# Emitting each group's work in two lanes, and splitting the mixed features on ScalarE and VectorE, in a one-layer streaming encoder

## The chip, the core and the metric

The kernel runs on one core of one Trainium2 chip. The metric is the device time of one execution in microseconds (us). Five engines work side by side, each through its own instructions in a fixed order: PE (TensorE, matmuls; its weight loads are listed as PEld), DVE (VectorE), ACT (ScalarE), POOL (GpSimd) and SP (SyncE, which here issues most DMAs). An instruction whose inputs aren't ready holds up all that stands behind it on its engine.

## What is computed

One layer with three attention groups that read the same normalised input through one projection and are merged by one output projection. In the prompt part 2048 rows of width 1024 are processed; 8 short sequences of 16 new rows each ("samples") attend into caches.

```python
def reference(...):
    qa, ka, va, ga, qb, kb, vb, gb, qm, gm = split(rmsnorm(x, g_pre) @ w_in)
    oa = band_attention(qa, ka, va, 8 chunks of 64 to the left, learned bias by distance)      # 6 heads
    ob = band_attention(qb, kb, vb, 2 chunks to the left, ALiBi, sinks)                        # 6 heads, 2 kv heads
    om = softmax(qm @ mk.T) @ mv      # 4 heads, 256 memory tokens, mk/mv = rmsnorm(mem, g_mem) @ w_mem_kv
    o = concat([oa * silu(ga), ob * silu(gb), om * silu(gm)]) @ w_out
    y = x + rmsnorm(o, g_post)
```

Outputs are y for prompt and samples and the new keys and values. All is in float32. Every matmul operand is split into a high part (rounded to the matmul's format) and a low part (the rest), and a product is three matmuls: high by high, high by low and low by high.

## The kernel before

The prompt is worked on in four groups of 512 rows (g = 0 to 3; group 0 also carries the 128 sample rows). For each group the kernel projects the normalised columns `xn` into queries, keys, gates (`psT`, matmuls of 512 columns) and values (`psN`, 256 columns), computes attention a pair of heads at a time, multiplies each result with its gate into the mixed features `mo`, splits these into high and low part in `sh` (`mixhl`), and projects them out (`psN<-whl,sh`). Products with weights (`psT`, `psN`) are called dense here.

Attention of a pair of heads goes in steps over several engines. PE makes scores (`sa` for A, `sb_` for B, `sm` for M), DVE adds the bias and takes the row's extreme (L727, L798, L643), ACT takes the exponential (L729, L800, L648), DVE the reciprocal and the scaling (L731 and L732, L805 and L809, L650 and L653), PE transposes (`pt`, L247), ACT and DVE split the transposed weights into `sh` (L208, L209), PE multiplies with the values (`oa`, `ob`, `om`, L260), and ACT and DVE merge the two halves (`sums`, L267, L268). POOL applies the gate (L631).

PSUM is shared out by pools: two banks for dense products, one score tile of two banks, three tiles for transposes, one for attention outputs. So a second score tile waits until DVE or ACT has read the first.

The order of a group is written out by hand as a string of steps in `ORDERS`, each one a whole block: V (values), Pa and Pb (projections of a pair of heads), Aa, Ab and M (attention of a pair), Sa and Sb (samples), K (keys of B), X (reload of context), F (normalise, add and store the group before), N and L (scales and rows of the next group), Q (its M queries). After the string, at the group's end, come the split of the mixed features and the four quarters of the output projection, with the next group's M attention ahead of them in the text. A scheduler then orders each engine's instructions, with the place in the text as priority: where the instruction of the earlier block must wait, ready instructions of a later block go first, as far as buffers allow.

Weights arrive by DMA in `wraw`; ACT makes the high part of each (L139) and DVE and POOL in turn subtract it (L140). The mixed features are split by DVE and POOL:

```python
def split_mixed(dst, i, fs, src):
    dve.tensor_copy(dst[:, i, 0, fs], src)                                                      # L890
    pool.tensor_tensor(dst[:, i, 1, fs], src, dst[:, i, 0, fs].bitcast(F32), ALU.subtract)     # L891
```

`mixhl` lies over the keys, the values and part of the transposed weights in `sh`, so most of the split must wait until the group's attention has read them. In group 3 the first two quarters of the output projection leave out feature block 2 (the third A pair) and so start before that pair is done; in the code they stand after all attention.

In `split_q` (L214 to L220) a high part of the queries is also copied to the other half of the partitions: for head 0 by DVE, for head 1 by ACT (L220).

## Time and profile before

| | us |
|---|---|
| median of 3 runs | 1191.94 |
| lowest and highest | 1188.3 and 1194.71 |
| the profiled execution | 1191.06 |
| span of its trace, first to last instruction | 1189.3 |

| engine | busy us | share of the span |
|---|---|---|
| PE | 1132.3 | 95% |
| DVE | 838.6 | 71% |
| ACT | 690.3 | 58% |
| POOL | 351.4 | 30% |

A busy PE isn't a PE at its peak, since matmuls overlap. What can be read directly is the time in which PE is idle: 57 us of the span. The profile's chain of work that ended last is 71% PE and 17% DVE. The groups' ends lie near 330, 620, 890 and 1130 us.

### The profile page before, as it was taken

To read this page: it belongs to the slowest core of one execution; us is meant where nothing else is said; L and a number is where in the kernel's file an instruction comes from. 1 tells how busy PE (TensorE), PEld (TensorE's weight loads), DVE (VectorE), ACT (ScalarE), POOL (GpSimd) and SP (SyncE) were. 2 spreads that over 40 slices of the span, in tenths; PEclk is the share of its full clock that TensorE was granted. 3 is DMA by queue.
4 is the path that set the end of the run, shared out by engine and by line. 5 is a ranking of instruction groups with operands and counts; after the bars stand their busy time and mean duration, and the time that the engine had idled before them with its cause. 6 is when DMAs were issued, how large, how long until landed. Compare 5 with 4: busy or idle time off the path is not lost.

```text
span 1189.3 us, 20990 instructions
## 1 busy us (share of the span) xinstructions
PE 1132.3 (95%) x7794; PEld 1019.2 (86%) x7794; DVE 838.6 (71%) x1915; ACT 690.3 (58%) x1611; POOL 351.4 (30%) x280
## 2 busy tenths in 40 slices
PE   7999999998899999999989999999989998999897
PEld 6989898996689978898878988898778987988797
DVE  7849666777873547779997337679996336679965
ACT  7646565665634655558665455557764445567652
POOL 4212111111441651213333552122333451221541
PEclk9999999999989999999999999999999998999999
DMA  7772643525522683243311593334321471332213
GB/s 266 249 248 86 196 147 100 209 70 191 198 72 72 211 314 113 94 125 109 118 58 37 165 349 115 95 115 127 117 59 36 155 263 63 122 98 86 90 55 106
DMA packets 62238, 163.43 MB, mean 137 GB/s; under 512 B 8108, under 2 KB 19378, under 8 KB 62136
## 3 DMA queue, kind: packets, MB, share of 16 engines
q1 hardware_dynamic: 58392, 152.66, 38.6%
q0 software_dynamic: 3744, 9.44, 2.8%
q8 instruction: 61, 1.00, 0.3%
q14 instruction: 41, 0.34, 0.1%
HBM read 140.95 MB, written 23.48 MB: 138 GB/s over the span
## 4 chain that ended last, share of the span: by engine, by line
PE 71%; DVE 17%; ACT 4%; issue 3%; DMA 2%; POOL 1%; SPq 0%; DVEq 0%; POOLq 0%; ACTq 0%
PE psT L191 32%; PE psN L202 21%; PE pt L247 4%; PE oa L260 3%; PE sa L241 3%; DVE sh L209 3%; DVE sba L727 1%; DVE whl L140 1%; DVE sbm L653 1%; DVE sbb L809 1%; DVE sbb L798 1%; PE ss L358 1%; ACT whl L139 1%; PE ob L260 1%; PE so L392 1%
## 5 line engine op out<-in xcount | busy, mean ns | idle before, releaser
L191 PE MATMUL psT<-xn,whl 128*128 128x512 f32 (+2 forms) x2400 | 530.6, 370 | 11.9 <-ACT whl L139 7.4
L191 PEld LDWEIGHTS psT<-xn,whl 128*128 128x128 f32 x2400 | 409.7, 192 | 74.0 <-ACT whl L139 7.6
L140 POOL TENSOR_TENSOR whl<-wraw,whl 128x1024 fp32r<-128x1024 f32 x63 | 152.3, 2417 | 353.0 <-ACT whl L139 323.1
L202 PE MATMUL psN<-whl,sh 128*128 128x256 f32 x1296 | 162.1, 282 | 1.5 <-POOL sh L891 1.3
L202 PEld LDWEIGHTS psN<-whl,sh 128*128 128x128 f32 x1296 | 156.3, 189 | 3.4 <-POOL sh L891 1.5
L139 ACT ACTIVATE whl<-wraw 128x1024 fp32r<-128x1024 f32 (+1 forms) x132 | 138.0, 1047 | 31.0 <-PE psN L202 13.5
L202 PE MATMUL psN<-whl,xn 128*128 128x256 f32 x1080 | 142.9, 283 | 3.4 <-ACT stgN L618 1.1
L202 PEld LDWEIGHTS psN<-whl,xn 128*128 128x128 f32 x1080 | 133.1, 189 | 7.5 <-issue 1.6
L209 DVE TENSOR_TENSOR sh<-pt,sh 128x512 fp32r<-128x512 f32 (+2 forms) x206 | 123.8, 626 | 20.5 <-ACT sh L208 19.4
L208 ACT ACTIVATE sh<-pt 128x512 fp32r<-128x512 f32 (+2 forms) x206 | 104.4, 547 | 38.4 <-PE pt L247 32.5
L729 ACT ACTIVATE sba<-sba,sta 128x640 f32<-128x640 f32 (+4 forms) x96 | 73.1, 762 | 65.9 <-DVE sta L727 64.4
L140 DVE TENSOR_TENSOR whl<-wraw,whl 128x1024 fp32r<-128x1024 f32 (+1 forms) x69 | 99.0, 1435 | 16.4 <-ACT whl L139 15.9
L631 POOL TENSOR_TENSOR mo<-sums,gr 128x256 f32<-128x256 f32 (+1 forms) x44 | 44.8, 1019 | 187.8 <-DVE sums L268 179.9
L727 DVE CUSTOM_DVE_ANT_0 sba<-sa,nbA 128x640 f32<-128x640 f32 (+4 forms) x96 | 70.6, 735 | 31.3 <-PE sa L241 30.7
L260 PE MATMUL oa<-sh 128*128 128x256 f32 (+1 forms) x504 | 81.5, 283 | 10.9 <-DVE sh L209 7.6
L260 PEld LDWEIGHTS oa<-sh 128*128 128x128 f32 x504 | 71.1, 191 | 17.1 <-DVE sh L209 9.8
L497 DVE TENSOR_TENSOR mo<-psN,gpost 128x256 f32<-128x256 f32 x52 | 22.0, 424 | 74.2 <-ACT junk L496 74.1
L247 PE MATMUL pt<-ident,sba 128*128 128x128 f32 x420 | 66.6, 278 | 3.4 <-DVE sba L732 3.2
L800 ACT ACTIVATE sbb<-sbb,stb 128x256 f32<-128x256 f32 (+1 forms) x96 | 47.2, 493 | 27.4 <-DVE stb L798 27.2
L732 DVE TENSOR_SCALAR sba<-sba,sta 128x640 f32<-128x640 f32 (+4 forms) x96 | 59.9, 624 | 2.6
L496 ACT ACTIVATE junk<-psN 128x256 bf16<-128x256 f32 x52 | 20.0, 384 | 62.3 <-PE psN L202 62.1
L247 PEld LDWEIGHTS pt<-ident,sba 128*128 128x128 f32 x420 | 48.9, 142 | 7.1 <-DVE sba L732 4.2
(282 smaller groups left out, 1629.2 us busy)
## 6 DMA issues: line engine op xcount, KB each, us to landing
wraw<-in_wt SPq DMA_DIRECT2D x128, 512.0 KB, 3.8
xr<-in_x_p SPq DMA_DIRECT2D x16, 512.0 KB, 5.8
nbA<-skew_d SPq DMA_DIRECT2D x24, 320.0 KB, 3.3
vta<-in_cva SPq DMA_DIRECT2D x12, 512.0 KB, 4.5
xt<-in_x_p SPq DMA_DIRECT2D x12, 512.0 KB, 5.2
out_y_p<-mo SPq DMA_DIRECT2D x12, 512.0 KB, 4.8
vctx<-sh SPq DMA_DIRECT2D x9, 512.0 KB, 5.8
kctx<-sh SPq DMA_DIRECT2D x9, 512.0 KB, 4.0
```

The lines of the kernel that those rows point to most:

```text
L139: act.activation(hl[:, 0, m], raw[:, m], AF.Copy)
L140: eng.tensor_tensor(hl[:, 1, m], raw[:, m], hl[:, 0, m].bitcast(F32), ALU.subtract)
L191: pe.matmul(ps[:, :n], w[:, a, k * 128:(k + 1) * 128], src[:, b, k, c0:c0 + n], start=(i == 0), stop=(i == 23))
L202: pe.matmul(ps[:, :256], stat(a, k), w[:, b, (k % 4) * 256:(k % 4 + 1) * 256], start=(k == ks[0] and i == 0), stop=(k == ks[-1] and i == 2))
L208: act.activation(hi, src, AF.Copy)
L209: eng.tensor_tensor(lo, src, hi.bitcast(F32), ALU.subtract)
L247: pe.transpose(pt[:, i * 128:(i + 1) * 128], b, ident)
L260: pe.matmul(o[:, oc:oc + w], v, pt[:, part, c:c + w], start=(first and i == 0), stop=(i == n - 1), skip_group_check=True)
L727: dve.tensor_tensor_reduce(sb[:, :nk], s[:, c0:c0 + nk], nb[h][:, 640 - nk:], 1.0, 3.0e38, ALU.add, ALU.min, st[:, e:e + 1])
L729: act.activation(sb[:, :nk], sb[:, :nk], AF.Exp, bias=st[:, e:e + 1], scale=-1.0, accum_out=st[:, 2 + e:3 + e])
L732: dve.tensor_scalar(sb[:, :nk], sb[:, :nk], st[:, 4 + e:5 + e], 0.5, ALU.mult, ALU.mult)
L800: act.activation(dst, dst, AF.Exp, bias=st[:, i:i + 1], scale=-1.0, accum_out=st[:, 4 + i:5 + i])
```

## The change

1. Steps become generators that yield after a few instructions: a `psT` product after every 6 matmuls, a `psN` product after half its matmuls. A group's steps are given in two strings, `DENSE` and `ATTENTION`, and a loop emits them as two lanes: the dense lane gets a piece when its sum of costs is at most `PACE` = 0.3 of the attention lane's, or when attention has to wait for a step in `AFTER`. This changes the order of the text, and so the scheduler's priorities.
2. Attention goes head by head: `weigh` (scores to scaled weights) of one head, and beside it up to three pieces of `combine` (transposes, values, merge) of the head before. For A, head 0's merge is now emitted before head 1's transposes; before, both heads' merges came after both.
3. The output projection of a group (O0 to O3) becomes the start of the next group's dense lane. In group 3 the two early quarters (E0) follow the last projection Pa2 in the dense lane, beside the last attention pair.
4. `split_mixed` uses ACT for the high part and DVE for the subtraction. POOL has no part in it.
5. `split_q` copies both heads by ACT.
6. Buffers: bias tiles `nb` 2 to 3, weight tiles `sb` 5 to 6, gate slots 2 and 3 laid out apart, and `mom` (M features) a tile of its own, no longer the fifth row tile of `mo`.

The matmuls are the same 7521 in both programs, and so is the number of DMAs on SP (410).

```diff
-ORDERS = ("M0 M1 V0 Pa0 Sa0 Aa0 Pa1 Pb0 Aa1 K0 V1 Sb0 N0 Sa1 Ab0 Pb1 Ab1 Sb1 Pb2 Ab2 Pa2 Sb2 Sa2 Aa2 L0 Q0 Q1 C0",
-          "V0 F0 F1 M0 X0 Pa0 M1 Aa0 X1 Pa1 N0 Aa1 Pb0 K0 Pb1 V1 Ab0 Pb2 Ab1 Ab2 C0 Pa2 X2 L0 Aa2 Q0 Q1",
...
+DENSE = ("V0 Pa0 Pa1 V1 Pb0 K0 N0 Pb1 Pb2 Pa2 L0 Q0 Q1 C0",
+         "O0 O1 O2 O3 F0 F1 V0 X0 Pa0 Pa1 N0 Pb0 X1 K0 V1 Pb1 X2 Pb2 Pa2 L0 Q0 C0 Q1",
...
+         "O0 O1 O2 O3 F0 V0 X0 Pa0 Pa1 Pb0 X1 K0 V1 Pb1 X2 Pb2 Pa2 E0")
+ATTENTION = ("M0 M1 Sa0 Aa0 Sa1 Aa1 Sb0 Ab0 Sb1 Ab1 Sb2 Ab2 Sa2 Aa2",
+             "M0 M1 Aa0 Aa1 Ab0 Ab1 Ab2 Aa2",
...
+PACE = 0.3
+PIECE = 6
...
-    nbp = ctx.enter_context(tc.tile_pool(name="nbp", bufs=2))
-    sbp = ctx.enter_context(tc.tile_pool(name="sbp", bufs=5))
+    nbp = ctx.enter_context(tc.tile_pool(name="nbp", bufs=3))
+    sbp = ctx.enter_context(tc.tile_pool(name="sbp", bufs=6))
...
-            (act.copy if h else dve.tensor_copy)(q[x, h, c], q[m, h, c].bitcast(F32))
+            act.copy(q[x, h, c], q[m, h, c].bitcast(F32))
...
         def split_mixed(dst, i, fs, src):
-            dve.tensor_copy(dst[:, i, 0, fs], src)
-            pool.tensor_tensor(dst[:, i, 1, fs], src, dst[:, i, 0, fs].bitcast(F32), ALU.subtract)
+            act.activation(dst[:, i, 0, fs], src, AF.Copy)
+            dve.tensor_tensor(dst[:, i, 1, fs], src, dst[:, i, 0, fs].bitcast(F32), ALU.subtract)
...
+        lanes = [dense(), attention()]
+        spent, waits = [0, 0], [(), ()]
+        while any(lanes):
+            ready = [lanes[k] is not None and done.issuperset(waits[k]) for k in range(2)]
+            assert any(ready), (g, waits)
+            k = 0 if ready[0] and (not ready[1] or spent[0] <= PACE * spent[1]) else 1
+            got = next(lanes[k], None)
+            waits[k] = ()
+            if got is None:
+                lanes[k] = None
+            elif isinstance(got, (tuple, list)):
+                waits[k] = got
+            else:
+                spent[k] += got
```

What the scheduler makes of it is seen in the order of the instructions on each engine. First place: PE at the end of group 1, where its last attention pair (A, `sa` and `oa`) meets the output projection. Before, this stands there after the last dense matmuls (`psT`), and it goes on in this way for 16 more rows, to the first `psN<-whl,sh`; from the `psT` to there it is 94 matmuls of attention:

```order
L191 MATMUL psT<-xn,whl 128x512 x17
L260 MATMUL oa<-sh 128x256
L241 MATMUL sa<-sh,qr 128x320 x4
L260 MATMUL oa<-sh 128x256 x4
L247 MATMUL pt<-ident,sba 128x128 x4
L260 MATMUL oa<-sh 128x256 x3
L260 MATMUL oa<-sh 128x128 x4
L247 MATMUL pt<-ident,sba 128x128 x6
L241 MATMUL sa<-sh,qr 128x320 x4
L260 MATMUL oa<-sh 128x256 x5
```

With the change, from the last `psT` to the first `psN`, whole:

```order
L213 MATMUL psT<-xn,whl 128x512
L273 MATMUL pt<-ident,sba 128x128 x10
L267 MATMUL sm<-mK,qr 128x256 x8
L286 MATMUL oa<-sh 128x256 x8
L286 MATMUL oa<-sh 128x128 x4
L273 MATMUL pt<-ident,sba 128x128 x8
L267 MATMUL sm<-mK,qr 128x256 x8
L273 MATMUL pt<-ident,sba 128x128 x2
L286 MATMUL oa<-sh 128x256 x8
L286 MATMUL oa<-sh 128x128 x4
L226 MATMUL psN<-whl,sh 128x256 x25
```

The run of attention without a dense matmul between is 60 long where it was 94; the last scores of the A pair now stand ahead of it. The end of group 2 shows the same 60.

Second place: PE where group 3's last B pair (`ob`) meets its last A pair. Before, `psN<-whl,xn` being values or an early quarter of the output projection:

```order
L260 MATMUL ob<-sh 128x256 x6
L260 MATMUL ob<-sh 128x128 x2
L260 MATMUL ob<-sh,bv 128x128 x2
L241 MATMUL sa<-sh,qr 128x320 x4
L247 MATMUL pt<-ident,sba 128x128 x3
L241 MATMUL sa<-sh,qr 128x320 x4
L202 MATMUL psN<-whl,xn 128x256 x6
L260 MATMUL ob<-sh 128x256 x6
L260 MATMUL ob<-sh 128x128 x2
L260 MATMUL ob<-sh,bv 128x128 x2
L241 MATMUL sa<-sh,qr 128x320 x4
L247 MATMUL pt<-ident,sba 128x128 x7
```

With the change:

```order
L286 MATMUL ob<-sh,bv 128x128 x2
L226 MATMUL psN<-whl,xn 128x256 x6
L267 MATMUL sa<-sh,qr 128x320 x4
L226 MATMUL psN<-whl,xn 128x256 x6
L267 MATMUL sa<-sh,qr 128x320 x4
L273 MATMUL pt<-ident,sba 128x128 x3
L226 MATMUL psN<-whl,xn 128x256
L267 MATMUL sa<-sh,qr 128x320 x4
L226 MATMUL psN<-whl,xn 128x256 x15
L273 MATMUL pt<-ident,sba 128x128 x7
L226 MATMUL psN<-whl,xn 128x256 x14
```

The last B head is over before the A pair's scores begin, and dense matmuls stand between their steps: 42 in the first 15 rows after it, where 6 stood in 23 rows.

Third place: DVE at the end of group 1. Before, the casts of `split_mixed` (their subtractions stand on POOL), among the scalings of M's weights (`sbm`):

```order
L890 CAST sh<-mo 128x768 x2
L650 RECIPROCAL stm<-stm 128x2
L653 TENSOR_SCALAR sbm<-sbm,stm 128x256 x2
L209 TENSOR_TENSOR sh<-pt,sh 128x512
L653 TENSOR_SCALAR sbm<-sbm,stm 128x256 x2
```

With the change:

```order
L926 TENSOR_TENSOR sh<-mo,sh 128x768
L926 TENSOR_TENSOR sh<-mom,sh 128x256
L235 TENSOR_TENSOR sh<-pt,sh 128x512
L926 TENSOR_TENSOR sh<-mom,sh 128x256
L235 TENSOR_TENSOR sh<-pt,sh 128x512
L926 TENSOR_TENSOR sh<-mom,sh 128x256
L294 TENSOR_TENSOR sums<-oa,sums 64x256
L679 TENSOR_REDUCE stm<-sm 128x4
L926 TENSOR_TENSOR sh<-mo,sh 128x768 x2
L686 RECIPROCAL stm<-stm 128x2
L689 TENSOR_SCALAR sbm<-sbm,stm 128x256 x2
```

The subtractions now stand on DVE between the steps of attention, the last two ahead of a scaling of `sbm`; POOL's list has none.

## Rows read from the trace of the kernel before

**Rows 1.** The page's part 1: busy us, share of the span, instructions of each engine.

```profile
PE 1132.3 (95%) x7794; PEld 1019.2 (86%) x7794; DVE 838.6 (71%) x1915; ACT 690.3 (58%) x1611; POOL 351.4 (30%) x280
```

**Rows 2.** Stretches: from:to, length, busy us and instructions by engine, granted clock, DMA.

```profile
core 0: us, PE busy (x) PEld busy (x) DVE busy (x) ACT busy (x) POOL busy (x), PEclk, DMA share, GB/s
...
280.00:340.00 60.00, 51.42 (x330) 36.95 (x329) 47.70 (x107) 32.34 (x77) 27.39 (x24) 0.89 0.55 189
340.00:560.00 220.00, 219.09 (x1467) 199.76 (x1466) 138.69 (x305) 123.83 (x280) 67.12 (x46) 1.00 0.43 143
560.00:640.00 80.00, 72.32 (x469) 64.31 (x468) 74.36 (x156) 51.77 (x129) 28.72 (x26) 0.98 0.24 72
...
820.00:905.00 85.00, 75.79 (x484) 66.43 (x483) 81.19 (x176) 57.51 (x143) 30.59 (x28) 1.00 0.27 84
...
985.00:1000.00 15.00, 11.45 (x45) 9.04 (x44) 11.39 (x22) 7.54 (x15) 2.36 (x1) 0.77 0.22 71
...
1100.00:1136.00 36.00, 31.07 (x191) 26.96 (x190) 33.97 (x76) 23.26 (x50) 19.00 (x18) 0.95 0.23 75
```

**Rows 3.** PE in order of time, end of group 1: start, length, instruction, [idle before <-releaser].

```profile
596.09 4.12 PE L191 MATMUL psT<-xn,whl 128*128 128x512 f32 x17
...
610.95 0.35 PE L260 MATMUL oa<-sh 128*128 128x256 f32 x1 [1.52 <-DVE sums L268]
...
614.84 0.36 PE L202 MATMUL psN<-whl,sh 128*128 128x256 f32 x1
...
616.20 0.74 PE L260 MATMUL oa<-sh 128*128 128x256 f32 x4 [0.76 <-DVE sh L209]
...
621.82 0.30 PE L247 MATMUL pt<-ident,sbm 128*128 128x128 f32 x1 [0.57 <-DVE sbm L653]
...
630.25 0.33 PE L247 MATMUL pt<-ident,sbm 128*128 128x128 f32 x1 [0.97 <-DVE sbm L653]
632.05 0.90 PE L247 MATMUL pt<-ident,sbm 128*128 128x128 f32 x3 [1.48 <-DVE sbm L653]
```

**Rows 4.** DVE and POOL in order of time, the same place.

```profile
613.44 2.11 DVE L653 TENSOR_SCALAR sbm<-sbm,stm 128x256 f32<-128x256 f32 x2
...
616.07 0.60 DVE L653 TENSOR_SCALAR sbm<-sbm,stm 128x256 f32<-128x256 f32 x2
...
628.27 3.73 DVE L653 TENSOR_SCALAR sbm<-sbm,stm 128x256 f32<-128x256 f32 x2
...
613.11 2.02 POOL L891 TENSOR_TENSOR sh<-mo,sh 128x768 fp32r<-128x768 f32 x1 [1.30 <-PE pt L247]
...
627.97 3.88 POOL L891 TENSOR_TENSOR sh<-mo,sh 128x768 fp32r<-128x768 f32 x2 [0.68 <-DVE sh L890]
```

**Rows 5.** The subtraction from a transpose in PSUM, one line: min/median/max ns.

```profile
L209 DVE TENSOR_TENSOR sh<-pt,sh x206: 407/682/694, 99.9 to 1148.3; 128x512 fp32r<-128x512 f32 x82, 128x256 fp32r<-128x256 f32 x18, 128x384 fp32r<-128x384 f32 x3
```

**Rows 6.** Groups of like instructions: count, busy us, mean ns, idle before.

```profile
L220 DVE CAST qr<-qr 64x512 fp32r<-64x512 f32 x16 | 11.1, 691 | 0.5
L220 ACT CAST qr<-qr 64x512 fp32r<-64x512 f32 x16 | 9.9, 619 | 0.5
L890 DVE CAST sh<-mo 128x1024 fp32r<-128x1024 f32 x5 | 3.3, 699 | 1.1 <-POOL mo L631 1.1
L891 POOL TENSOR_TENSOR sh<-mo,sh 128x1024 fp32r<-128x1024 f32 x5 | 13.7, 2750 | 2.6 <-DVE sh L890 2.5
L139 ACT ACTIVATE whl<-wraw 128x1024 fp32r<-128x1024 f32 x130 | 136.8, 1054 | 29.1 <-PE psN L202 13.5 <-DMA wraw<-in_wt 7.7 <-PE psT L191 6.7
L140 DVE TENSOR_TENSOR whl<-wraw,whl 128x1024 fp32r<-128x1024 f32 x67 | 97.6, 1457 | 15.1 <-ACT whl L139 14.7
L140 POOL TENSOR_TENSOR whl<-wraw,whl 128x1024 fp32r<-128x1024 f32 x63 | 152.3, 2417 | 353.0 <-ACT whl L139 323.1 <-issue 25.6 <-PE sa L241 2.9
```

**Rows 7.** All engines in order of time, group 3, a stall away from a group's end.

```profile
991.66 2.36 POOL L140 TENSOR_TENSOR whl<-wraw,whl 128x1024 fp32r<-128x1024 f32 x1 [11.56 <-ACT whl L139]
...
991.98 2.40 DVE L732 TENSOR_SCALAR sba<-sba,sta 128x640 f32<-128x640 f32 x1
...
994.43 1.76 PE L247 MATMUL pt<-ident,sba 128*128 128x128 f32 x7 [1.67 <-DVE sba L732]
```

More of the change, by code (lines that the diff above doesn't have):

```diff
@@ L182, in loaded, with run @@
         return xk
+    def run(steps):
+        while True:
+            try:
+                next(steps)
+            except StopIteration as end:
+                return end.value
     def project_T(w, src, c0, n, ps=None):
@@ L758, in attn_a @@
-                sums = cp_.tile([128, 512], F32, tag="sums", name="sums")
-                for h in range(2):
-                    merge(o, h, 256 * h, sums, 256)
-                gate(pr, i0 * 128, 256, sums, G)
+                    s = p_s.tile([128, 1024], F32, tag="s", name="sa")
+                    scores(s, q, h, i * 128, segs)
+                    e = i - i0
+                    sb = sbp.tile([128, 640], F32, tag="sb", name="sba")
+                    dve.tensor_tensor_reduce(sb[:, :nk], s[:, c0:c0 + nk], nb[h][:, 640 - nk:], 1.0,
+                                             3.0e38, ALU.add, ALU.min, st[:, e:e + 1])
@@ L763, in project_b @@
+            return [(weigh(i0, h), combine(i0, h)) for i0 in (0, 2) for h in range(2)]
         def project_b(j0):
[L764 removed]
+            q, Q = yield from block_q(g, 3 + j0)
+            return q, Q, (yield from block_g(g, 3 + j0))
         def sample_b(j0, Q, G, ksm, vsm):
@@ L823, in attn_b @@
                     first = False
-                merge(o, h, 0, sums, 512)
-            gate(3 + j0, 0, 512, sums, G)
+                    yield 600
+                merge(o, h, 0, held["sums"], 512)
+                if h:
+                    gate(3 + j0, 0, 512, held["sums"], G)
+            return [(weigh(h), combine(h)) for h in range(2)]
         if g == 0:
@@ new lines, in out_quarter @@
+        def out_quarter(c):
+            nrt = 5 if g == 1 else 4
+            if c == 0:
+                turn["m"] = 1
+                for i in range(nrt):
+                    if g == 1:
+                        split_mixed(mixhl, i, slice(0, KB), mo[:, i])
+                    else:
+                        split_mixed(mixhl, i, slice(0, 6), mo[:, i, :6])
+                        split_mixed(mixhl, i, slice(6, KB), mom[:, :, i])
+                kept["post"] = gains()
+            ws = [weights("o", c, r) for r in range(2)]
+            for i in range(nrt):
+                yield from project_out(ws, c, i, *kept["post"])
+            if c == 3:
+                turn["m"] = 0
@@ new lines, in units, with attention, pieces @@
+        def units(what, j):
+            if what == "M":
+                return attn_m(j, *qg[j])
+            if what == "Aa":
+                return attn_a(j, pa[j][1], pa[j][3], at[j], vslots[j], vc[j])
+            if what == "Ab":
+                return attn_b(j, pb[j][0], pb[j][2], v3, bctx)
+            if what == "Sa":
+                return [(iter(()), sample_a(j, *pa[j][2:], pa[j][0], vsm[j]))]
+            return [(iter(()), sample_b(j, *pb[j][1:], kept["ksm"], vsm[3]))]
+        def attention():
+            last = None
+            def pieces(n):
+                nonlocal last
+                for _ in range(n):
+                    if last:
+                        cost = next(last[0], None)
+                        if cost is None:
+                            done.update(last[1])
+                            last = None
+                        else:
+                            yield cost
+            for step in ATTENTION[g].split():
+                while not done.issuperset(after(step)):
+                    if last:
+                        yield from pieces(1)
+                    else:
+                        yield after(step)
+                parts = units(step[:-1], int(step[-1]))
+                for i, (first, second) in enumerate(parts):
+                    for cost in first:
+                        yield cost
+                        yield from pieces(3)
+                    while last:
+                        yield from pieces(1)
+                    last = (second, [(g, step)] if i == len(parts) - 1 else [])
+            while last:
+                yield from pieces(1)
```

332 lines of the change are left out of this document (173 added, 159 removed), and 5 rows, old and new, of tables (ATTENTION, DENSE, ORDERS).

## The prediction

> **What bounds the kernel now.** I read the page's busy times first: PE is busy 95% of the span and DVE 71% [rows 1], and the 7521 matmuls stay, so a gain can only come out of PE's idle 57 us (1189.3 - 1132.3) and out of the time at the lower granted clock. Then I cut the span into stretches [rows 2]. From 340 to 560 us PE idles 0.9 of 220 us: away from the groups' ends nothing is to be had. The ends are different: idle 8.6 us in 280 to 340, 7.7 in 560 to 640, 9.2 in 820 to 905 and 4.9 in 1100 to 1136, **30.4 us** in all. In the same stretches the granted clock is 0.89, 0.98, 1.00 and 0.95 [rows 2]; as time at the half level (1.2 of 2.4 GHz), lost if PE had work all along, that is 0.11 x 60 + 0.02 x 80 + 0.05 x 36 = **10 us**. So about 40 us is the most that better group ends can give. Another 3.6 us of idle and 3.5 us of clock (0.23 x 15) lie in 985 to 1000, inside group 3.
>
> Third, PE in order of time at one end [rows 3]. From the last dense run, which begins at 596.09, to the first `psN` at 614.84 PE has attention alone, 94 matmuls in chains that go through DVE and ACT; five waits there and just after it make 5.3 of the 7.7 us: 1.52 for a merge (`sums`), 0.76 for a subtraction of transposed weights, and 0.57 + 0.97 + 1.48 = 3.0 for scaled M weights (`sbm`, L653). What holds DVE? It is busy 74.4 of 80 us there and 81.2 of 85 at the next end [rows 2]: full. And some of that is no work: two L653 take 0.60 us when POOL is quiet, 2.11 us while a `split_mixed` subtraction (L891) runs on POOL from 613.11, and 3.73 us beside the two of 627.97 [rows 4]. DVE work that reads a transpose out of PSUM isn't touched: 206 of them, none over 694 ns [rows 5]. So **a POOL subtraction stretches DVE work between SBUF tiles**, and at the group's end that is the work on which PE waits.
>
> **The change part by part.**
>
> *Split of the mixed features.* 17 row tiles of 1024 columns' worth. POOL loses five subtractions of 2750 ns and the narrower ones [rows 6], and nothing takes their place there; POOL isn't waited for much, so that is worth nothing by itself. DVE loses the cast (699 ns a tile) and gets a subtraction of the size of its weight subtraction, 1457 ns a tile [rows 6]: +0.76 x 17 = +13 us of DVE, some 3 us at each end. ACT gets a copy like its weight copy, 1054 ns a tile [rows 6]: 18 us on an engine that is busy 58% [rows 1]. The chain of one tile gets shorter, 1.05 + 1.46 = 2.5 us for 0.70 + 2.75 = 3.4, and four or five tiles in a row no longer queue on POOL. Against the +3 us at an end stand the stretched L653 that go away: 2.11 - 0.60 and 3.73 - 0.60 are 4.6 us for two rows alone [rows 4]. Queued behind the new copies on ACT are exponentials and copies of transposes, behind the new subtractions on DVE the next `sbm`; if nothing covers them, one tile's 2.5 us at each of four ends is 10 us, and if all is covered 0. I take 0, since the first tiles are ready before the last attention matmuls and their 24 dense matmuls stand behind them on PE.
>
> *Query copies to ACT.* 40 copies change engine: 16 wide ones are 11.1 us on DVE and 9.9 on ACT [rows 6]. With the same rates for the rest DVE loses some 22 us and ACT gains 21. In the quiet stretches this is free (ACT 124 of 220 us busy [rows 2]), at the ends it is 2 to 3 us off the full engine. With the split, DVE comes out at -22 + 13 = -9 us over the span, and its stretched work beside that.
>
> *Two lanes.* By the order, the macro position of attention hardly moves (scores stand within 10 us of dense work of where they stood), but the ends do: the run of attention without dense work is 60 matmuls where it was 94, 0.64 of it, at the ends of groups 1 and 2; in group 3 the last pairs have 42 dense matmuls among 40 of attention where 6 stood among 76. A's first head is merged before its second head's values, so the 1.52 us wait for `sums` [rows 3] halves. Nothing is paid for the pieces: a switch from dense to attention matmuls and back already happens all over 340 to 560 us, at 0.9 us idle [rows 2]. Added waits: POOL's gate of the last pair now stands behind the next bias tile's two fills, which wait for a DMA; behind the gate are the subtractions on DVE of tiles 2 and 3. I price that at 0, because the fills stood in that place before too; one more wait of a tile costs the 2.5 us above.
>
> *Buffers.* A third bias tile and a sixth weight tile let attention start earlier; between 0 and what the ends have left. I take 0 beside the order's gain.
>
> **The sum.** End of group 1, 7.7 us: `sbm` 3.0 goes whole, `sums` 0.8 of 1.5, of the remaining 3.1 a share of 0.36 (1 - 0.64) is 1.1: 4.9 saved, 64%. End of group 2 by the same share: 5.9 of 9.2. End of group 0: half its first 20 us is sample attention, which changes less; I take half, 4.3 of 8.6. End of group 3: two thirds of 4.9, 3.3, since dense work now stands in the gap. Idle saved: 18.4 us. Of the 10 us of clock I take half, 5, because the clock fell after PE had idled and more than half of the idle goes. Together **23.4 us**, against the profiled execution's own 1191.06: 1167.7, so **1168 us**. The median of the runs is 0.9 us above that execution, which is inside its spread.
>
> **The Trainium skill on POOL and DVE.** The trace shows L653 at 0.60, 2.11 and 3.73 us a pair by what POOL does [rows 4], and a PSUM operand immune [rows 5]. The Trainium skill, "SBUF — State Buffer", section on SBUF's two separate sides, states that VectorE and GpSimd share a port pair under an exclusive lock, held for a whole instruction, and that a VectorE operation with two SBUF inputs also loses against a GpSimd one that reads SBUF. The rows agree: the L653 of 613.44 ends 0.4 us after the L891 of 613.11. The rule speaks against one part of the change, since the new DVE subtraction has two SBUF inputs and POOL's weight subtractions read SBUF; by it the sum would be rival 2's 1187 instead of 1168.
>
> **The rivals.**
>
> 1. *Only the split counts.* The scheduler had already mixed dense work and attention, so lanes change the text more than the order. Then only what L891 stretched goes: 3.0 us at the ends of groups 1 and 2 each, as much together at the others, and a fifth of the clock, 2 us: 11 us, **1180 us**. For it: scores stand where they stood. Against: 60 for 94.
>
> 2. *The new subtraction is itself held up by POOL's weight subtractions.* They stay, 63 of 2417 ns [rows 6], and one of them held an L732 for 2.40 us and PE behind it for 1.67 [rows 7]. If at each end two of the subtractions lose 2.4 us and PE pays them, that is 4 x 2 x 2.4 = 19 us back: 1168 + 19 = 1187, **about no change**. For it: DVE is full at the ends. Against: dense matmuls stand behind the first tiles. The skill's rule above is a reason for it.
>
> 3. *Slower: finer mixing puts more attention in the way of weight subtractions.* PE takes its list in order, and a matmul of attention that waits for a held DVE step holds up the dense work behind it. Before, one such hit in 985 to 1000 us cost 3.6 us of idle and up to 3.5 of clock [rows 2, 7]. With single heads instead of pairs, less stands between a score and the use of its weights; group 3 now has `sa` twice in a row and `oa` at once behind it. At some 5 us a hit, five more hits eat the gain and six to seven make it slower than before by 0.5%: 1168 + 32 = **1200 us** with six to seven of the 63 subtractions. For it: 63 chances. Against: from 340 to 560 us, with its share of those 63, nothing of the kind shows.
>
> 4. *More than I give.* Attention that starts earlier leaves dense work for the ends, and all 40 us but 2 go, with 5 of the 985 stall: 1191 - 38 - 5 = **1148 us**.
>
> **How the numbers follow.** Forecast 1168: 0.53. Rival 1: 0.18, rival 2: 0.10, rival 3: 0.10, rival 4: 0.09. About 0.5% (6 us) is what a measurement of this kernel can tell from no change. Of the forecast 0.51 lies beyond it on the faster side, of rival 1 0.14 of 0.18, of rival 2 0.04 of 0.10, all of rival 4: faster 0.78; rival 3 leaves 0.08 on the slower side; the rest, 0.14, is the same. The range goes from rival 4's 1148, less 2 for its own spread, to the median of before, 1192: outside are rival 3 and a little of rival 4 and 2, some 0.15.
>
> **What would show it.** Right: PE idle under 14 us in the four ends together, no `sbm` scaling above 1 us beside a split, DVE's total near 825 us or below, ACT near 730, POOL near 300; the same quiet middle. Only the split: the long waits for `sbm` gone and those for `sums` and transposed weights as before. Rival 2: the subtractions of `split_mixed` at twice 1.4 us, with a weight subtraction on POOL beside them. Rival 3: new PE waits of over 1 us for `sba` or `sbb` in the middle of groups. Wrong altogether: PE idles away from the ends for weights or for a DMA.

## The result, and the profile after

The changed kernel takes **1179.5 us** (median; 1177.1 to 1180.0), the kernel before 1192.5 in the same comparison: a ratio of 0.988, 95% interval 0.986 to 0.990, or 13 us less. The prediction said 1168 in a range of 1146 to 1192: the direction holds and the range does, but the gain is 13 us where the sum said 23.4. The profiled execution took 1177.05 us, its span is 1175.3; those of before are 1191.06 and 1189.3.

Page of the changed kernel, part 1, to be read against [rows 1]:

```profile
PE 1126.3 (96%) x7794; PEld 1019.6 (87%) x7794; DVE 810.9 (69%) x1875; ACT 729.4 (62%) x1688; POOL 301.1 (26%) x243
```

PE's idle time fell from 57.0 to 49.0 us, and its busy time by 6.0 for the same matmuls. The totals that were forecast for the others (825 or less, 730, 300) came. Stretches of the changed kernel, to be read against [rows 2] (its groups end some microseconds earlier, so the last one is moved); columns are time, length, busy us and count by engine, granted clock, DMA share and rate:

```profile
core 0: us, PE busy (x) PEld busy (x) DVE busy (x) ACT busy (x) POOL busy (x), PEclk, DMA share, GB/s
0.00:80.00 80.00, 66.52 (x471) 61.86 (x471) 51.98 (x97) 49.67 (x101) 22.86 (x26) 0.96 0.72 239
...
205.00:220.00 15.00, 10.88 (x65) 8.87 (x64) 12.68 (x43) 10.71 (x32) 5.01 (x4) 0.77 0.50 160
280.00:340.00 60.00, 53.58 (x354) 41.04 (x353) 47.34 (x111) 38.99 (x87) 17.87 (x21) 0.94 0.53 180
340.00:560.00 220.00, 218.51 (x1474) 200.26 (x1473) 137.74 (x304) 129.32 (x288) 62.05 (x43) 1.00 0.42 141
560.00:640.00 80.00, 74.62 (x501) 66.96 (x500) 71.83 (x159) 62.52 (x151) 20.31 (x20) 1.00 0.24 77
...
820.00:905.00 85.00, 80.72 (x540) 72.40 (x539) 76.83 (x177) 66.34 (x161) 22.36 (x22) 1.00 0.27 87
...
1095.00:1130.00 35.00, 32.45 (x218) 30.11 (x218) 29.12 (x56) 27.11 (x59) 8.55 (x4) 0.90 0.28 93
```

And two stretches of the kernel before that the prediction did not look at:

```profile
0.00:80.00 80.00, 70.37 (x523) 65.06 (x524) 56.27 (x107) 50.10 (x102) 23.66 (x25) 0.98 0.75 246
205.00:220.00 15.00, 14.87 (x127) 12.21 (x128) 7.50 (x18) 6.89 (x16) 4.78 (x2) 1.00 0.87 317
```

The four ends did get better: idle 6.4, 5.4, 4.3 and 2.6 us, 18.6 for 30.4. But the first 80 us idle 13.5 for 9.6, and 205 to 220 us, which was full, idles 4.1 and runs at 0.77 of the clock.

PE at the end of group 1 in the changed kernel, to be read against [rows 3]:

```profile
567.12 1.22 PE L267 MATMUL sb__6329<-sh,xn 128*128 128x256 f32 x8 [1.00 <-DVE stb L856]
...
590.52 5.87 PE L213 MATMUL psT<-xn,whl 128*128 128x512 f32 x24 [0.66 <-DVE qr L245]
...
613.11 1.72 PE L273 MATMUL pt<-ident,sba 128*128 128x128 f32 x8 [1.29 <-DVE sh L235]
...
618.91 2.98 PE L226 MATMUL psN<-whl,sh 128*128 128x256 f32 x23 [1.06 <-DVE sh L926]
621.74 1.03 PE L273 MATMUL pt<-ident,sbm 128*128 128x128 f32 x8
```

The waits for scaled M weights (`sbm`, 3.0 us) and for the merge (1.5) are gone whole. Other waits stand in their place: for the bias step of B's scores (L856), for the split of queries (L245, another 0.55 at 570 us), for transposed weights, and for the subtraction of the mixed features (L926).

Stretches of equal length don't hold equal work, so I also summed, over all matmuls, how much longer each start-to-start distance is than the usual one of its form where PE is full (234 ns for 512 columns, 175 for 384, 147 for 320, 118 for 256, 110 for 128), and cut that sum at equal amounts of work. It holds idle time and clock together; small negative entries are sample attention, whose matmuls are shorter than that. Lost us:

| stretch (us in before) | before | after | split_alone | lanes_old_split | late_bias | late_head_pairs |
|---|---|---|---|---|---|---|
| start (0 to 92) | 5.5 | 10.7 | 5.5 | 9.5 | 4.1 | 4.4 |
| rest of group 0 (to 230) | -2.0 | 0.5 | -1.0 | 0.3 | 0.0 | 2.0 |
| end of group 0 (to 340) | 10.4 | 4.2 | 12.1 | 5.5 | 4.0 | 9.6 |
| group 1 (to 561) | 1.5 | 1.9 | -0.1 | 4.4 | 3.5 | 0.4 |
| end of group 1 (to 653) | 12.0 | 8.4 | 9.5 | 19.0 | 8.4 | 3.7 |
| group 2 (to 815) | 1.9 | 0.3 | 2.5 | 0.2 | 1.0 | 0.9 |
| end of group 2 (to 928) | 12.5 | 7.2 | 12.4 | 13.5 | 7.9 | 3.9 |
| group 3, first part (to 1036) | 8.5 | 3.7 | 7.9 | 3.8 | 3.8 | 3.8 |
| group 3, second part (to 1096) | -0.1 | 2.0 | -0.1 | 2.0 | 2.0 | 1.8 |
| end of group 3 | 8.9 | 6.4 | 9.4 | 7.3 | 5.9 | 5.2 |
| all | 59.0 | 45.3 | 58.2 | 65.5 | 40.6 | 35.8 |

13.7 of the 14.0 us between the spans are in it. The ends give 6.2 + 3.6 + 5.3 + 2.5 = 17.6 us, the stall of [rows 7] and its neighbourhood 4.8; the start takes 5.2, the rest of group 0 2.5 and the second part of group 3 2.1 back. The columns other than the first two are experiments.

### The profile page after: what moved, and what is told of

Read it like the earlier page. It is cut to its first block, busy times and chain, and to the rows that moved or that the text cites. A ratio compares the mean times of both kernels' runs of the same rounds, so it can differ in the third digit from the quotient of the medians.

```text
span 1175.3 us, 20987 instructions
## 1 busy us (share of the span) xinstructions
PE 1126.3 (96%) x7794; PEld 1019.6 (87%) x7794; DVE 810.9 (69%) x1875; ACT 729.4 (62%) x1688; POOL 301.1 (26%) x243
## 4 chain that ended last, share of the span: by engine, by line
PE 69%; DVE 10%; issue 8%; ACT 8%; DMA 3%; POOL 2%; SPq 1%; DVEq 0%; POOLq 0%; ACTq 0%
PE psT L213 31%; PE psN L226 20%; PE pt L273 4%; PE oa L286 4%; PE sa L267 4%; DVE sh L235 2%; ACT whl L153 1%; POOL whl L154 1%; PE ob L286 1%; DMA xt<-in_x_p 1%; DVE whl L154 1%; PE ss L384 1%; PE om L286 1%; DVE sbm L689 1%; PE so L420 1%
## 5 line engine op out<-in xcount | busy, mean ns | idle before, releaser
L213 PE MATMUL psT<-xn,whl 128*128 128x512 f32 (+2 forms) x2400 | 522.1, 367 | 13.7 <-ACT whl L153 5.7
L775 ACT ACTIVATE sba<-sba,sta 128x640 f32<-128x640 f32 (+2 forms) x96 | 73.1, 762 | 57.8 <-DVE sta L773 57.3
L154 DVE TENSOR_TENSOR whl<-wraw,whl 128x1024 fp32r<-128x1024 f32 (+1 forms) x69 | 94.9, 1375 | 19.4 <-ACT whl L153 18.7
L665 POOL TENSOR_TENSOR mo<-sums,gr 128x256 f32<-128x256 f32 (+1 forms) x38 | 37.6, 989 | 234.7 <-DVE sums L294 208.8
L773 DVE CUSTOM_DVE_ANT_0 sba<-sa,nbA 128x640 f32<-128x640 f32 (+2 forms) x96 | 70.7, 737 | 28.8 <-PE sa L267 27.8
L286 PE MATMUL oa<-sh 128*128 128x256 f32 (+1 forms) x504 | 75.1, 281 | 1.8 <-DVE sh L235 0.9
L286 PEld LDWEIGHTS oa<-sh 128*128 128x128 f32 x504 | 68.4, 192 | 5.0 <-DVE sh L235 1.9
L778 DVE TENSOR_SCALAR sba<-sba,sta 128x640 f32<-128x640 f32 (+2 forms) x96 | 59.4, 619 | 2.7
L267 PE MATMUL sa<-sh,qr 128*128 128x320 f32 (+2 forms) x240 | 52.0, 327 | 4.4 <-DVE sta L773 2.3
```

The costliest lines, as they stand in the source:

```text
L154: eng.tensor_tensor(hl[:, 1, m], raw[:, m], hl[:, 0, m].bitcast(F32), ALU.subtract)
L213: pe.matmul(ps[:, :n], w[:, a, k * 128:(k + 1) * 128], src[:, b, k, c0:c0 + n], start=(i == 0), stop=(i == 23))
L267: pe.matmul(out[:, c:c + n], q[:, part, qc:qc + 128], kt[:, h, kc:kc + n], start=part == h, stop=part != h)
L286: pe.matmul(o[:, oc:oc + w], v, pt[:, part, c:c + w], start=(first and i == 0), stop=(i == n - 1), skip_group_check=True)
L773: dve.tensor_tensor_reduce(sb[:, :nk], s[:, c0:c0 + nk], nb[h][:, 640 - nk:], 1.0, 3.0e38, ALU.add, ALU.min, st[:, e:e + 1])
L775: act.activation(sb[:, :nk], sb[:, :nk], AF.Exp, bias=st[:, e:e + 1], scale=-1.0, accum_out=st[:, 2 + e:3 + e])
```

## The experiments

Every ratio is against the kernel before, run on the same chip beside it (its medians were 1191.1 to 1193.0).

| run | median us | ratio, 95% interval |
|---|---|---|
| split_alone | 1190.1 | 0.998 (0.996 to 1.000) |
| lanes_old_split | 1196.4 | 1.004 (1.002 to 1.005) |
| all_but_lanes | 1189.3 | 0.997 (0.995 to 1.000) |
| all_but_lanes_late | 1182.8 | 0.992 (0.990 to 0.994) |
| two_bias_tiles | 1185.4 | 0.994 (0.991 to 0.996) |
| two_bias_idle_pool | 1193.4 | 1.000 (0.999 to 1.002) |
| late_bias | 1172.9 | 0.984 (0.980 to 0.987) |
| late_bias_one_weight | 1182.4 | 0.991 (0.988 to 0.995) |
| vector_query_copies | 1187.6 | 0.996 (0.993 to 0.998) |
| dense_first | 1246.3 | 1.045 (1.042 to 1.047) |
| head_pairs | 1177.9 | 0.988 (0.986 to 0.990) |
| late_head_pairs | 1170.2 | 0.982 (0.980 to 0.984) |

An edit also makes the scheduler place other instructions anew. With equal neighbours taken as one row, PE's order is the changed kernel's to the last row in late_bias; it differs in some 210 of 1129 rows in lanes_old_split, 330 in two_bias_tiles, 800 in vector_query_copies and 890 in head_pairs. Against the 1205 rows of the kernel before, split_alone differs in some 130 and all_but_lanes in 640. Where it differs, the time is that of the edit and of the new order together.

### Split or order?

The split alone, in the kernel before:

```diff
-            dve.tensor_copy(dst[:, i, 0, fs], src)
-            pool.tensor_tensor(dst[:, i, 1, fs], src, dst[:, i, 0, fs].bitcast(F32), ALU.subtract)
+            act.activation(dst[:, i, 0, fs], src, AF.Copy)
+            dve.tensor_tensor(dst[:, i, 1, fs], src, dst[:, i, 0, fs].bitcast(F32), ALU.subtract)
```

> The kernel before with one thing of the change: mixed features are copied by ScalarE and subtracted by VectorE. Theory A (most of the gain is that POOL no longer stretches VectorE at the groups' ends): 11 us of the 13 come with this edit alone, about 1181 us, and no scaling of M weights (L653) takes over 1 us beside a split. Theory B (the lanes give the gain, the split is incidental): 1189 to 1193 us, since VectorE gains 13 us of work where it is full. If both add, about half each: 1186 us.

Measured 1190.1 us: 2.5 us, near theory B, though the mechanism of theory A is there. Line L653 alone in the ends of groups 1 and 2, first of before, then of split_alone (columns: stretch, length, DVE busy and count, clock, DMA):

```profile
560.00:640.00 80.00, 11.91 (x16) 0.98 0.24 72
820.00:905.00 85.00, 8.70 (x16) 1.00 0.27 84
```

```profile
560.00:640.00 80.00, 4.75 (x16) 1.00 0.23 73
820.00:905.00 85.00, 4.74 (x16) 0.96 0.25 83
```

The 16 scalings shrink by 7.2 and 4.0 us, to 0.30 us each. In time that brings 2.5 us at the first end and 0.1 at the second (table). PE at the first end of split_alone, to be read against [rows 3], and the whole second end, to be read against [rows 2]:

```profile
612.67 0.35 PE L260 MATMUL oa<-sh 128*128 128x256 f32 x1 [1.45 <-DVE sums L268]
...
628.61 0.33 PE L247 MATMUL pt<-ident,sbm 128*128 128x128 f32 x1 [0.89 <-DVE sbm L653]
...
632.38 4.63 PE L202 MATMUL psN<-whl,sh 128*128 128x256 f32 x37 [1.11 <-DVE sh L891]
```

```profile
820.00:905.00 85.00, 78.37 (x488) 69.33 (x487) 78.81 (x173) 60.70 (x148) 19.58 (x20) 0.96 0.25 83
```

At the first end the waits for `sbm` fall from 3.0 to 0.9 us, but the wait for the merge stands (1.45 for 1.52), and a dense product now waits 1.11 us for the split on DVE. At the second end PE idles 6.6 us for 9.2, and the granted clock is 0.96 where it was 1.00: what the waits gave, the clock took. The held steps were real, and at the first end what stood behind them was late too.

The lanes with the old split are the same edit reversed, in the changed kernel:

> The changed kernel with the split of mixed features put back to VectorE's copy and POOL's subtraction; lanes, pieces, buffers and query copies stay. Theory A: the 11 us of the split are lost, about 1190 us, with scalings of M weights of 2 to 4 us beside POOL's subtractions at the ends of groups 1 and 2. Theory B: 1179 to 1182 us. Both add: about 1186 us.

Measured 1196.4 us, slower than the kernel before and 17 us slower than the changed kernel, more than either theory gave. The loss sits at the ends of groups 1 and 2 (19.0 and 13.5 us for 8.4 and 7.2). POOL, DVE and PE in order of time at the first:

```profile
639.88 3.87 POOL L926 TENSOR_TENSOR sh<-mo,sh 128x768 fp32r<-128x768 f32 x2 [2.62 <-DVE sh L925]
...
640.19 1.89 DVE L689 TENSOR_SCALAR sbm<-sbm,stm 128x256 f32<-128x256 f32 x1
...
642.66 1.24 DVE L689 TENSOR_SCALAR sbm<-sbm,stm 128x256 f32<-128x256 f32 x1
...
642.79 0.65 PE L273 MATMUL pt<-ident,sbm 128*128 128x128 f32 x4 [2.55 <-DVE sh L235]
```

Two subtractions on POOL, two scalings held (1.89 and 1.24 us for 0.35), and PE idle for 2.55. So beside the rest of the change the split is worth 17 us, and alone 2.5: they don't add. The rest holds the copies and the buffers as well as the lanes, and no run has those with neither lanes nor split; which part of the rest the split needs isn't shown.

The old order of the text with all the rest of the change:

```diff
 # before, beside the split as above
-            (act.copy if h else dve.tensor_copy)(q[x, h, c], q[m, h, c].bitcast(F32))
+            act.copy(q[x, h, c], q[m, h, c].bitcast(F32))
-    nbp = ctx.enter_context(tc.tile_pool(name="nbp", bufs=2))
-    sbp = ctx.enter_context(tc.tile_pool(name="sbp", bufs=5))
+    nbp = ctx.enter_context(tc.tile_pool(name="nbp", bufs=3))
+    sbp = ctx.enter_context(tc.tile_pool(name="sbp", bufs=6))
```

> The kernel before, in its own order of the text, with everything of the change but the lanes, the heads and the gate slot: split by ScalarE and VectorE, both query copies on ScalarE, three bias tiles, six weight tiles. Theory T (order and split act together, neither does much alone): 1186 to 1190 us, and the ends of groups 1 and 2 still lose 8 to 10 us each in waits and clock. Rival (relief of VectorE and the buffers are the gain, the order of the text does nothing): 1179 to 1182 us.

Measured 1189.3 us, theory T's. The two ends lose 8.0 and 9.5 us there, where the changed kernel loses 8.4 and 7.2.

### The start

In the changed kernel ACT, SP, POOL and PE do this at 48 to 60 us:

```profile
48.30 1.06 ACT L153 ACTIVATE whl<-wraw 128x1024 fp32r<-128x1024 f32 x1 [0.48 <-PE psT L213]
...
51.90 0.90 SPq L757 DMA_DIRECT2D nbA<-skew_d  x2
...
55.48 0.15 POOL L758 MEMSET nbA<- 64x64 f32 x1 [10.11 <-DMA nbA<-skew_d]
...
55.90 2.34 POOL L154 TENSOR_TENSOR whl<-wraw,whl 128x1024 fp32r<-128x1024 f32 x1
...
58.30 6.26 PE L226 MATMUL psN<-whl,sh 128*128 128x256 f32 x34 [4.42 <-POOL whl L154]
```

And in the kernel before:

```profile
48.26 0.34 SPq L706 DMA_DIRECT2D nbA<-skew_d  x1
...
51.21 0.14 POOL L707 MEMSET nbA<- 64x64 f32 x1 [4.48 <-DMA nbA<-skew_d]
...
51.63 2.39 POOL L140 TENSOR_TENSOR whl<-wraw,whl 128x1024 fp32r<-128x1024 f32 x1
...
53.44 5.92 PE L202 MATMUL psN<-whl,sh 128*128 128x256 f32 x48
```

In the changed kernel ACT has the weight's high part ready at 49.4 us, but POOL subtracts it only at 55.90: ahead of that subtraction POOL has to fill a corner of a bias tile, and for that it waits for the tile's load, which SP issues at 51.90. In the kernel before the fill stands there too, but the load goes at 48.26. With two tiles one bias load stands between two sets of eight small loads of the samples' bias (`nbs`); with a third tile SP's list has two bias loads, behind all sixteen. (The expectations below also speak of the weight's load behind them on SP. That load, at 52.89, is another weight's; the one that PE waits for had landed before ACT took it at 48.30.) The first step of attention that reads one of the two tiles (L773) starts at 122 us. First the tile taken back (`bufs=3` to `bufs=2` for nbp, nothing else):

> The changed kernel with two bias tiles instead of three. In the changed kernel PE waits 4.6 us at 53.9 to 58.3 us for a weight subtraction on POOL: that weight's load stands behind two loads of bias tiles on SyncE, and POOL waits for them to do its fills first; then 6.8 us at half clock follow. Theory S (the third tile lets the second bias load in ahead of the weight): the wait and the clock drop vanish, 4.6 + 3.4 = 8 us at most, some 6 by the running sum of losses, so about 1173 us if nothing else moves. Rival (the third tile is what lets attention start early at the ends of groups): the start gains as much, but the ends lose, 1179 us or more.

Measured 1185.4 us, the rival's side: the start loses 6.7 us, not 10.7, but the rest of group 0 5.2 for 0.5, its end 7.9 for 4.2, group 1 5.3 for 1.9. So the third tile seems to earn its place away from the start, though PE's order moved too and this profiled execution is 2.7 us slower than its median. It stays, and the two loads wait:

```diff
                         t = nbp.tile([128, 640], F32, tag="nb", name="nbA")
+                        if g == 0 and pr == 0:
+                            dve.tensor_copy(t[:, 0:8], mV[:, 1, 1, 0:8].bitcast(F32))
                         sp.dma_start(out=t, in_=toeplitz(2 * pr + hh, 128, 0, 640))
```

> The changed kernel, three bias tiles, with one thing added: the first pair's two bias loads of group 0 wait until the memory values are there (a copy of 8 columns into the tile ahead of each load), so that they no longer stand ahead of the weight on SyncE nor hold POOL ahead of its subtraction. The order of PE is the same to the last row. Theory S (these two loads make the wait of 4.6 us at 53.9 to 58.3 and the half clock behind it): the wait goes, some 6 us by the running sum of losses, 1173 us. Rival (the weight is late of itself, its load being asked for at 52.9 us because a buffer comes free only then): the wait stays at 3 us or more, 1177 to 1180 us.

Measured 1172.9 us, as theory S said. POOL, SP and PE:

```profile
48.55 2.40 POOL L154 TENSOR_TENSOR whl<-wraw,whl 128x1024 fp32r<-128x1024 f32 x1 [4.06 <-ACT whl L153]
...
61.46 0.38 SPq L759 DMA_DIRECT2D nbA<-skew_d  x1
...
51.08 5.92 PE L226 MATMUL psN<-whl,sh 128*128 128x256 f32 x48
```

POOL subtracts the weight as soon as ACT has its high part, the bias load goes 10 us later, the wait is gone, and the first 80 us run at a clock of 1.00. The same edit in the old order of the text:

> The run with everything but the lanes, with the late bias loads of group 0 as well; PE's order is unchanged. There the third bias tile made the same loss at the start as in the changed kernel: PE waits 5.4 us at 58.8 us. Theory S (the third tile costs 5 to 6 us in either order of the text): 1183 to 1184 us, 10 to 11 us above the same edit in the changed kernel, which is then what the lanes are worth with all else equal. Rival (the wait is one that only the lanes' text makes costly): 1187 to 1190 us.

Measured 1182.8 us, 6.5 less than all_but_lanes. So the third tile costs some 6 us at the start in either order (by the ratios 5.2 and 6.6; there PE waited 5.22 us for the same subtraction), and with that out of the way the lanes, with their single heads and gate slots, are worth 0.992 to 0.984, some 10 us. Where these lie is not where the prediction put them: all_but_lanes_late loses 9.6, 7.4, 7.9 and 9.1 us at the four ends, late_bias 4.0, 8.4, 7.9 and 5.9. The lanes gain at the ends of groups 0 and 3, and 3.7 us in the middles of groups 1 and 2, but nothing at the ends of groups 1 and 2 (in the pair without the late loads -0.4 and 2.3 us there).

### POOL's hold, with nobody waiting for the result

In the kernel with two bias tiles (three leave no room in SBUF for its result) POOL does work that nobody reads:

```diff
             dve.tensor_tensor(dst[:, i, 1, fs], src, dst[:, i, 0, fs].bitcast(F32), ALU.subtract)
+            if not isinstance(fs, int):
+                hi = dst[:, i, 0, fs].bitcast(F32)
+                pool.tensor_tensor(spill[:, fs], hi, hi, ALU.subtract)
```

> The kernel with two bias tiles, and beside it a subtraction on POOL of the size of each split (the high half minus itself, from SBUF to SBUF), whose result nothing reads: POOL's work of the old split without anyone who waits for it. Theory L (work of POOL between SBUF tiles stretches VectorE's work between SBUF tiles, wait or no wait): scalings of M weights and the split's subtractions beside them take 2 to 4 us instead of 0.6 and 1.2, and the time rises by 3 us at each of two to four ends, 6 to 11 us over the run with two bias tiles. Rival (what POOL cost before was only the wait for its result): the same time within 2 us as the run with two bias tiles.

Measured 1193.4 us, 8.0 above two_bias_tiles, with PE's order the same up to 1130 us and some 20 of 1100 rows different behind that. The same place, the end of group 0, without and then with that work:

```profile
330.52 2.36 DVE L926 TENSOR_TENSOR sh<-mo,sh 128x1024 fp32r<-128x1024 f32 x2 [0.23 <-ACT sh L925]
...
335.91 0.50 PE L213 MATMUL psT<-xn,whl 128*128 128x512 f32 x1 [1.69 <-DVE gr L599]
```

```profile
335.36 4.06 DVE L927 TENSOR_TENSOR sh<-mo,sh 128x1024 fp32r<-128x1024 f32 x2 [0.75 <-ACT sh L926]
335.47 5.70 POOL L930 TENSOR_TENSOR spill<-sh 128x1024 bf16<-128x1024 f32 x2 [0.78 <-ACT sh L926]
...
341.12 0.80 PE L214 MATMUL psT<-xn,whl 128*128 128x512 f32 x1 [5.17 <-DVE gr L600]
```

Two splits take 4.06 us instead of 2.36, the gate behind them is late, and PE waits 5.17 us instead of 1.69. The end of group 0 loses 16.6 us for 7.9, but some 5 of these 8.7 lie ahead of 335.5 us, where the first of the new subtractions starts, so they aren't its price. The ends of groups 1 and 2 lose the same within 0.6 us, though steps are held there as well (two scalings took 1.63 us for 0.62). So the hold is a fact without any wait for POOL's result, and a hold of this kind cost PE 3.5 us in one place and nothing in another. The Trainium skill, "SBUF — State Buffer", section on SBUF's two separate sides, states the rule (a lock on a shared port pair for the whole instruction); the traces agree, with 4.06 us for 2.36.

Next, one weight's subtraction taken off POOL. In the changed kernel it hits DVE here:

```profile
208.22 2.35 POOL L154 TENSOR_TENSOR whl<-wraw,whl 128x1024 fp32r<-128x1024 f32 x1 [1.06 <-ACT whl L153]
208.37 2.65 DVE L253 TENSOR_TENSOR sh<-cs,sh 64x128 fp32r<-64x128 f32 x2 [0.46 <-ACT sh L252]
...
210.76 0.50 PE L267 MATMUL sb__2521<-sh,qr 128*128 128x256 f32 x2 [2.03 <-DVE sh L253]
```

```diff
-        eng = (dve, pool)[turn["s"] % 2 if turn["s"] > 4 else 0]
+        eng = (dve, pool)[turn["s"] % 2 if turn["s"] > 4 and turn["s"] not in (23,) else 0]
```

> As the run with late bias loads, and one weight more (the 24th, whose subtraction on POOL runs from 208.2 to 210.6 us in the changed kernel) is subtracted by VectorE. In the changed kernel VectorE's L253 takes 2.65 us beside it where two take 0.6 elsewhere, PE waits 2.0 us for that and 1.8 us more until 213, and 6.8 us at half clock follow. Theory L (one weight subtraction on POOL in the wrong place costs some 5 us, the price that the prediction's third rival gave a hit): 3 to 5 us less than with late bias loads alone, about 1169 us. Rival (VectorE is the bound there, and 1.2 us more in its queue cost as much as the hold): the same within 1.5 us.

Measured 1182.4 us, 9.5 slower than late_bias: neither theory. At the place itself, and then at the end of group 0:

```profile
204.74 0.61 DVE L253 TENSOR_TENSOR sh<-cs,sh 64x128 fp32r<-64x128 f32 x2
205.08 0.50 PE L267 MATMUL sb__2523<-sh,qr 128*128 128x256 f32 x2 [1.04 <-DVE sh L253]
...
330.50 2.35 POOL L154 TENSOR_TENSOR whl<-wraw,whl 128x1024 fp32r<-128x1024 f32 x1 [1.10 <-PE oa L286]
...
331.35 2.58 DVE L928 TENSOR_TENSOR sh<-mo,sh 128x1024 fp32r<-128x1024 f32 x1 [0.55 <-ACT sh L927]
...
334.59 2.93 PE L213 MATMUL psT<-xn,whl 128*128 128x512 f32 x6 [4.77 <-DVE gr L599]
```

The hold is gone, and PE's wait there is 1.04 us for 2.03. But the order of PE differs from late_bias in some 230 rows, another weight subtraction came to run beside a split, and the end of group 0 lost 14.0 us for 4.0; the wait behind that split makes 4.0 of the 10 (4.77 us for 0.79). The run says little of the one weight; it shows that an edit of 1 us in this kernel can move 10.

### What in the lanes?

Some of it shows in the programs alone. With a pace of 0, 0.15 or 0.6 instead of 0.3, or pieces of 24 matmuls instead of 6, the order of instructions is the same row for row on every engine: neither number decides anything there. What may decide is that attention goes first whenever it is ready. The opposite (`PACE = 0.3` to `9.0`):

> The changed kernel with the pace of the lanes at 9 instead of 0.3: dense products go ahead of attention in the text as long as they are ready (any pace from 0 to 0.6 gives the same order of instructions as 0.3). The longest runs of attention without a dense matmul are then 99, 98 and 118 matmuls in groups 1, 2 and 3, where the changed kernel has 60, 60 and 34, and the kernel before 94, 94 and 55. Theory T (it is attention ahead of dense work, which leaves dense work for the groups' ends, that makes the lanes worth 10 us): these 10 us go, and group 3 loses more than before: 1190 to 1197 us, PE idle over 55 us. Rival (the smaller units and the split make the gain wherever they stand): 1179 to 1183 us.

Measured 1246.3 us, far beyond theory T. Its page and one stretch:

```profile
PE 1155.0 (93%) x7794; PEld 1037.2 (83%) x7794; DVE 814.5 (65%) x1875; ACT 733.7 (59%) x1688; POOL 301.5 (24%) x243
```

```profile
340.00:560.00 220.00, 209.24 (x1361) 189.83 (x1362) 128.30 (x244) 119.67 (x251) 58.80 (x43) 0.98 0.39 132
```

PE idles 90 us, and not at the ends alone: the quiet middle, 0.9 us idle in [rows 2], idles 10.8. In lost us, groups 1 and 2 lose 21.6 and 6.5 us ahead of their ends (1.9 and 0.3 in the changed kernel) and 16.8 and 14.8 at them. So dense work first is far worse than the order written by hand (1246 us for 1191): the run shows that the order decides much, but not why the lanes beat the old text. The next run puts the heads back together:

```diff
                 parts = units(step[:-1], int(step[-1]))
+                while last:
+                    yield from pieces(1)
+                if len(parts) > 1:
+                    parts = [tuple(chain(*x) for x in zip(*parts[a:a + 2])) for a in range(0, len(parts), 2)]
```

> The changed kernel with both heads of a unit weighed and then both combined, and each unit finished before the next begins, as in the kernel before; lanes and all else stay. The longest run of attention without a dense matmul is 43 matmuls, not 60. Theory R (by the prediction's own yardstick the length of that run sets the loss at an end): the ends of groups 1 and 2 lose a third less than in the changed kernel, 1175 to 1178 us. Rival H (single heads let PE go on with one head while VectorE weighs the other, and the yardstick counts the wrong thing): 1183 us or more, with more PE waits of over 1 us for scores and for scaled weights at the ends.

Measured 1177.9 us: the changed kernel's time, and theory R's just so. The ends of groups 1 and 2 lose 5.7 and 5.4 us for 8.4 and 7.2, a third and a quarter less, as the run's length of 43 for 60 says; the end of group 0 loses 10.3 for 4.2 and eats it. But the length isn't all that changed. In all_but_lanes_late the longest runs there are 63 and 87 matmuls and the ends lose 7.4 and 7.9 us; late_bias has 60 and 60 and loses 8.4 and 7.9. The yardstick is not borne out, and why head_pairs gains at these two ends stays open. With the late bias loads:

> The two edits that did no harm apart, together: late bias loads in group 0 (6.6 us faster than the changed kernel) and both heads of a unit at once (the same as the changed kernel within 2 us). PE's order is that of the run with head pairs. Theory (the two lie in different places and add): 1171 to 1173 us. Rival (what follows shifts against POOL's weight subtractions and loses it elsewhere): 1176 us or more.

Measured 1170.2 us: the best of all, though its interval and that of late_bias overlap. With PE's order that of head_pairs to the last row, the ends of groups 1 and 2 lose 3.7 and 3.9 us here for 5.7 and 5.4, so differences of 2 us between two profiles prove little. Last, the query copies back to DVE (that one line of all_but_lanes reversed):

> The changed kernel with half of the query copies put back to VectorE (22 us of its work over the run). Theory D (VectorE is full at the groups' ends, so 2 to 3 us there count): 3 to 6 us slower, 1182 to 1186 us. Rival (they lie in the quiet stretches, nothing counts): 1179 us within 2 us.

Measured 1187.6 us, 8 more than the changed kernel, somewhat over theory D. With some 800 rows of PE's order different, the copies' own price isn't separated from that of the new order. Its profiled execution was 4 us quicker than that median, so I read places from it and no sums: the end of group 2 loses 11.9 us for 7.2, and the stall of [rows 7] is back, with the same cast:

```profile
985.77 2.36 POOL L154 TENSOR_TENSOR whl<-wraw,whl 128x1024 fp32r<-128x1024 f32 x1 [11.56 <-ACT whl L153]
...
986.07 2.41 DVE L778 TENSOR_SCALAR sba<-sba,sta 128x640 f32<-128x640 f32 x1
...
989.13 0.74 PE L286 MATMUL oa<-sh 128*128 128x256 f32 x4 [2.15 <-DVE sh L235]
```

## Why the prediction was right, and why its size was not

- **Where the time is: right, with luck.** The ends of the groups give 17.6 us and next to nothing came from the middle. The stall at 985 us gives another 4.8; the sum had left it out, and nothing in the change aims at it.
- **The ends: 23.4 us forecast with the clock, 17.6 measured.** Group 0 gave 6.2, group 1 3.6, group 2 5.3, group 3 2.5. Idle alone went from 30.4 to 18.6 us, not below 14. Two terms came: at the end of group 1 the 3.0 us of `sbm` went whole, and so did the 1.5 for the merge, of which half was forecast. The step that failed is the share of 0.36 taken off all the rest there, by the length of attention's run (60 for 94): the rest went from 3.1 to 5.4 us, with 1.25 for the split, 1.2 for queries, 1.0 for the bias step of B's scores and 1.3 for transposed weights. The ends of groups 1 and 2 lose about as little without the lanes; what the lanes give lies at the ends of groups 0 and 3.
- **The third bias tile, priced at 0: wrong, and with the ends the largest miss.** It was looked at only as room for attention, and POOL's fills were priced at 0 because they had stood there before. They had, but the load that the fill waits for now goes 3.6 us later, and an urgent subtraction stands behind the fill: some 6 us in two orders of the text. Of a buffer that is added, the question to ask was what it moves in SP's and POOL's lists, and what stands behind that.
- **The clock, 5 us forecast: 1 measured.** Time at the half level is 34.2 us before and 32.5 after, and half of the difference counts. At the four ends it fell from 20.4 to 13.6 us, which is 3.4 us won; drops came anew behind the wait of 4.4 us at the start and those at 208 to 212 us (0.77 in the stretch). With late_bias 22.5 us are left.
- **The query copies: the direction right, the size open.** They were given 2 to 3 us at an end; undone the run takes 8 more, in part because a weight subtraction on POOL falls on a scaling again, and with another order on PE.
- **The split's cover, priced at 0: nearly right, in part by luck.** PE's dense products wait 2.0 us in all for the new subtractions, 1.06 of it at the end of group 1. Gates also queue behind the split's copies on ACT and its subtractions on DVE at the end of group 0. There PE waited 0.78 us in the changed kernel, 1.69 with two bias tiles, 4.77 and 5.17 where POOL ran beside the splits.
- **The rivals.** Rival 1 gave the measured time (1180) for a wrong reason: the split alone is 2.5 us, not 11, and the lanes do count, by 10. Rival 2 didn't come: the 13 subtractions of groups 0 to 2 that are 768 or 1024 wide took 1.23 us at most; in group 3 one was held (two took 3.24 us at 1111.4, the longer 2.77), while PE had dense matmuls. Rival 3's mechanism came once, at 208 us, and one such hit, that of 985, went; both by the way the order fell, which nothing in the change aims at.
- **The sum as it is.** By the ratios: the split, the copies and the buffers 0.992 with the start mended (10 us), the lanes from there to 0.984 (10 us), the start some 6.5 us back: 13. That the split and the rest don't add is shown; how the first 10 divide between split, copies and buffers stays open, and so does why the lanes gain where they do.
